# Three of four sums of weight blocks and one low part move from GpSimd to VectorE in the gate and up projection of layer 1

## The chip, the cores and the metric

The kernel runs on one core of a Trainium2 chip. A core has TensorE (matrix products into PSUM), VectorE and ScalarE (which read PSUM and SBUF), GpSimd (SBUF alone) and SyncE, whose queue issues the loads here. The metric is the device time of one execution in microseconds, the median of the timed runs. In the rows PE is TensorE, PEld its loading of weights, DVE is VectorE, ACT is ScalarE, POOL is GpSimd and SP is SyncE.

## The reference

A two-layer backbone over 512 latent tokens and 256 context tokens, model width 1024. Each layer has a mixer and a SwiGLU feed-forward part, both between norms and modulations. The change lies in the gate and up products of the second layer's feed-forward part, which exists for the latent tokens alone:

```
D_FF = 2816                     # 22 blocks of 128 columns
def swiglu(u, w_gate, w_up, w_down):
    return (jax.nn.silu(u @ w_gate) * (u @ w_up)) @ w_down
...
    f = swiglu(modulate(rms_norm(h, g_pre_ffn[i]), sh_f, sc_f), w_ffn_gate[i], w_ffn_up[i], w_ffn_down[i])
    h = h + gt_f * rms_norm(f, g_post_ffn[i])
```

## The kernel before

All products are in fp32 accuracy, made of three passes: each operand is split into a high part (a ScalarE copy to the rounded format, line 181) and a low part (operand minus high part, line 182, on VectorE unless another engine is given). The three passes are high by high, high by low and low by high (lines 197 to 199).

The gate and up products use Winograd's form of Strassen's scheme: for a pair of weight row blocks and a pair of token blocks, 7 products take the place of 8. The sums on the token side (tile `ub`) are made while the tokens are normalised (`norm_W`, `Winograd.add`, lines 1440 to 1475). The sums on the weight side are made in `gate_up`, `group`, for each two of the 22 column blocks, once for the gate weights (m = 0) and once for the up weights (m = 1): 22 groups, which take turns gate, up, gate, up. A group does this:

- two loads of 512 KB bring four blocks of weights, 128 rows by 512: a11, a12, a21, a22 (tile `raw_gu`, four buffers, so two groups);
- four sums of them: s1 = a21 + a22, s2 = s1 - a11, s4 = a12 - s2, s3 = a11 - a21 (tile `s`, four buffers in turn, so the sums of one group), lines 1556 to 1559, all on GpSimd;
- seven products, of a11, a12, s1, s4, s3, s2 and a22. For each the high part is made on ScalarE and the low part on VectorE; the low part of s3 alone is made on GpSimd. Each product is 4 x 3 matmuls;
- the products come out of PSUM by one ScalarE copy (line 1551) and seven additions on VectorE that read PSUM and SBUF (lines 1552 and 1562 to 1567);
- `done`: for the gate, ScalarE applies silu (line 1617); for the up weights GpSimd multiplies gate and up, two operations (line 1615).

The variable `n` is the number of columns of one product: 384 in layer 0 (768 tokens, six blocks, three pairs) and 256 in layer 1 (512 tokens, two pairs). `wide` is true for n <= 256, so in layer 1 alone; there two products share one PSUM bank.

The order on each queue isn't the order of the text. A planner simulates the engines with costs of its own and issues what is ready, earlier lines first. Each engine then runs its queue strictly in order, and a semaphore wait holds what stands behind it.

Of the kernel before, what the change touches and what calls it, by code (L numbers as in the profile page):

```python
# [155 lines left out]
ALU = mybir.AluOpType  # L156
# [7 lines left out]
def emit(tc, A):  # L164
    nc = tc.nc
    V, S, G, T = nc.vector, nc.scalar, nc.gpsimd, nc.tensor
# [29 lines left out]
    def mm3(out, wh, wl, xh, xl, start, stop):  # L196
        T.matmul(out, wh, xh, start=start, stop=False)  # L197
        T.matmul(out, wh, xl, start=False, stop=False)  # L198
        T.matmul(out, wl, xh, start=False, stop=stop)  # L199
# [220 lines left out]
    def pacc(name="pacc"):  # L420
        return bank_of(("g", "g", "g", "s", "s", "po"), name)

    def ptp(name="ptp"):
        return bank("v", name)

    def wraw(nm):
        return wp.tile([128, RK, 512], F32, tag="raw", name="raw_" + nm, bufs=RB)

    def wsplit(src, nm, lo_eng=None):
        hi, lo = [wp.tile([128, 512], F32R, tag=x_, name=f"{x_}_{nm}") for x_ in ("hi", "lo")]  # L430
        n = src.shape[1]
        split(hi[:, :n], lo[:, :n], src, lo_eng)
        return hi[:, :n], lo[:, :n]
# [1086 lines left out]
    def gate_up(U, pairs, wg, wu, place, done, lead):  # L1520


        n = pairs * 128
        wide = n <= 256
        v3 = lambda ap: ap.rearrange("p (i c) -> p i c", c=128)
        def group(f, m, w):
            def rows(f, n):
                raw = wraw("gu")
                nc.sync.dma_start(raw.rearrange("p (f j) c -> p f (j c)", f=n), w[f:f + n].rearrange("f p c -> p f c"))
                return [raw[:, i, :] for i in range(2 * n)]  # L1530

            a11, a12, *low = rows(f, RK // 2)
            banks = {}

            def prod(i, a, b, lo_eng=None):

                n_ = i // 2 if wide else i
                if n_ not in banks:
                    banks[n_] = ptp("st") if i == 6 and not wide else pacc("st")
                ps = banks[n_][:, i % 2 * 256:i % 2 * 256 + n] if wide else banks[n_][:, :n]  # L1540
                hi, lo = wsplit(a, "gu", lo_eng)
                for q in range(4):
                    ks = slice(q * 128, (q + 1) * 128)
                    uh_, ul_ = U.moving(b, q)
                    mm3(v3(ps), hi[:, ks], lo[:, ks], uh_, ul_, q == 0, q == 3)
                return v3(ps)

            p1, q_ = [v3(x) for x in U.sums_of_products()]
            c = place(f, m)
            P1, P2 = prod(0, a11, 0), prod(1, a12, 4)  # L1550
            S.activation(p1, P1, AF.Copy)
            V.tensor_tensor(c[0][0], p1, P2, ALU.add)
            yield
            a21, a22 = low or rows(f + 1, 1)
            s1, s2, s3, s4 = [U.sums.tile([128, 512], F32, tag="sum", name=f"s{i}", bufs=4) for i in range(4)]
            G.tensor_tensor(s1, a21, a22, ALU.add)  # L1556
            G.tensor_tensor(s2, s1, a11, ALU.subtract)
            G.tensor_tensor(s4, a12, s2, ALU.subtract)
            G.tensor_tensor(s3, a11, a21, ALU.subtract)
            P5, P3 = prod(3, s1, 1), prod(2, s4, 5)  # L1560
            P7, P6 = prod(4, s3, 2, G), prod(5, s2, 3)
            V.tensor_tensor(q_, p1, P6, ALU.add)
            V.tensor_tensor(p1, q_, P5, ALU.add)
            V.tensor_tensor(c[0][1], p1, P3, ALU.add)
            V.tensor_tensor(c[1][1], p1, P7, ALU.add)
            V.tensor_tensor(q_, q_, P7, ALU.add)
            V.tensor_tensor(c[1][0], q_, prod(6, a22, 6), ALU.add)
            done(f, m)

        lag = Lagged(lead)  # L1570
        for f in range(0, KF, 2):
            for m, w in enumerate((wg, wu)):
                with tc.issue_after(U.turned.ins) if 0 < f + m < lead else ExitStack():
                    lag.add(group(f, m, w))
                if f + m + 1 >= lead:
                    lag.flush()
# [644 lines left out]
```

## Time and profile before

| what | value |
|---|---|
| median of 3 runs | 2040.51 us |
| the three runs | 2040.86, 2040.51, 2028.3 us |
| the profiled execution | 2035.29 us |
| its span, first to last instruction | 2033.5 us |
| granted TensorE clock, mean | 0.955 |
| gate and up stage of layer 1 | about 1655 to 1905 us of the span |

The profile is one execution. Busy time counts an instruction from start to end, so it includes the time in which a started instruction is held up. The times of rows are microseconds from the start of the span.

### The profile page before, as it was taken

Reading aid. Unit: us, or ns where it says so; the run is one execution under the profiler, and the core shown is the slowest. Engines: PE = TensorE matmul, PEld = TensorE weight load, DVE = VectorE, ACT = ScalarE, POOL = GpSimd, SP = SyncE. Lnnn points to the kernel's source line nnn. Section 1 sums busy time; section 2 is a strip of 40 time slices with the busy share of each in tenths; the row PEclk is TensorE's granted clock in tenths of the full one; section 3 lists DMA queues with packets and bytes.
Section 4 is the critical chain, followed back from the end, with each engine's and each line's share of the span. In section 5 each row is a group of like instructions: output and inputs, shape, how many; then the busy total and the mean of one; then the engine's idle time right before and its main releaser. Section 6 shows DMA issues by size and latency. Waiting matters only on the chain. (4 is left out here: it accounts for less than half of the span.)

```text
span 2033.5 us, 33984 instructions
## 1 busy us (share of the span) xinstructions
PE 1844.2 (91%) x12852; PEld 1524.8 (75%) x12852; DVE 1449.5 (71%) x1973; ACT 962.5 (47%) x1806; POOL 1063.3 (52%) x936
## 2 busy tenths in 40 slices
PE   5989977888898969999999999889989969999998
PEld 3977754655566869999997777677755659999886
DVE  3687757667876696666666876887566679999754
ACT  3433456666864553333343235523455445444443
POOL 1276455344523376656548555656246358888201
PEclk8999988998999979999999889999999979999999
DMA  8255595655734613221227433586524202333331
GB/s 304 68 152 142 180 285 162 186 161 163 230 92 142 235 62 105 78 83 63 74 91 255 156 119 99 171 271 217 169 90 133 94 21 88 100 96 102 105 103 63
DMA packets 125728, 280.19 MB, mean 138 GB/s; under 512 B 12870, under 2 KB 43474, under 8 KB 125564
## 3 DMA queue, kind: packets, MB, share of 16 engines
q1 hardware_dynamic: 125564, 278.02, 43.5%
q8 instruction: 101, 1.65, 0.3%
q14 instruction: 63, 0.52, 0.1%
HBM read 226.14 MB, written 46.07 MB: 134 GB/s over the span
## 5 line engine op out<-in xcount | busy, mean ns | idle before, releaser
L197 PE MATMUL st<-ub,hi_gu 128*128 128x384 f32 (+1 forms) x1232 | 384.2, 312 | 18.0 <-ACT ub L181 18.0
L199 PE MATMUL st<-ub,lo_gu 128*128 128x384 f32 (+1 forms) x1232 | 385.5, 313 | 11.3 <-POOL lo_gu L182 9.5
L198 PE MATMUL st<-ub,hi_gu 128*128 128x384 f32 (+1 forms) x1232 | 384.0, 312 | 1.8 <-DVE ub L182 1.8
L197 PEld LDWEIGHTS st<-ub,hi_gu 128*128 128x128 f32 x1232 | 233.9, 190 | 18.9 <-ACT ub L181 18.9
L199 PEld LDWEIGHTS st<-ub,lo_gu 128*128 128x128 f32 x1232 | 233.7, 190 | 15.3 <-POOL lo_gu L182 11.6
L198 PEld LDWEIGHTS st<-ub,hi_gu 128*128 128x128 f32 x1232 | 233.8, 190 | 2.5 <-DVE ub L182 2.5
L181 ACT ACTIVATE hi_gu<-s 128x512 fp32r<-128x512 f32 x176 | 110.9, 631 | 191.0 <-PE st L198 141.8
L182 DVE TENSOR_TENSOR lo_gu<-raw_gu,hi_gu 128x512 fp32r<-128x512 f32 x132 | 161.5, 1237 | 39.9 <-ACT hi_gu L181 39.9
L182 DVE TENSOR_TENSOR lo_gu<-s,hi_gu 128x512 fp32r<-128x512 f32 x132 | 151.4, 1148 | 44.5 <-ACT hi_gu L181 44.1
L1649 PE MATMUL dn<-hi_wd,gh 128*128 128x512 f32 x440 | 174.5, 399 | 2.2 <-ACT gh L181 2.2
L1650 PE MATMUL dn<-lo_wd,gh 128*128 128x512 f32 x440 | 174.9, 398 | 0.8 <-DVE lo_wd L182 0.8
L1651 PE MATMUL dn<-hi_wd,gl 128*128 128x512 f32 x440 | 165.7, 403 | 6.1 <-POOL gl L182 5.1
L254 DVE SCALAR_TENSOR_TENSOR macc<-mraw,cs,macc 128x1024 f32<-128x1024 f32 x80 | 123.4, 1564 | 22.4 <-DMA mraw<-in_wmb_dram 13.5
L182 DVE TENSOR_TENSOR lo_wd<-raw_wd,hi_wd 128x512 fp32r<-128x512 f32 x110 | 99.4, 910 | 47.4 <-ACT hi_wd L181 47.3
L181 ACT ACTIVATE hi_gu<-raw_gu 128x512 fp32r<-128x512 f32 x132 | 81.8, 629 | 96.7 <-PE st L198 88.7
L1556 POOL TENSOR_TENSOR s<-raw_gu 128x512 f32<-128x512 f32 x44 | 57.3, 1302 | 133.0 <-DVE lo_gu L182 100.3
L181 ACT ACTIVATE gh<-g 128x512 fp32r<-128x512 f32 x76 | 47.6, 630 | 122.3 <-PE dn L1650 103.2
L860 ACT ACTIVATE P<-st 128x512 f32<-128x512 f32 x128 | 73.1, 596 | 67.2 <-PE st L199 28.3
L1651 PEld LDWEIGHTS dn<-hi_wd,gl 128*128 128x128 f32 x440 | 83.2, 191 | 28.3 <-POOL gl L182 7.9
L1649 PEld LDWEIGHTS dn<-hi_wd,gh 128*128 128x128 f32 x440 | 84.2, 191 | 22.4 <-ACT gh L181 2.7
L1650 PEld LDWEIGHTS dn<-lo_wd,gh 128*128 128x128 f32 x440 | 83.9, 191 | 20.8 <-DVE lo_wd L182 1.3
L1104 ACT ACTIVATE cu<-Y 64x512 f16<-64x512 f32 x120 | 70.7, 589 | 19.6 <-PE Y L1158 17.8
(539 smaller groups left out, 4917.8 us busy)
## 6 DMA issues: line engine op xcount, KB each, us to landing
mraw<-in_wmb_dram SPq DMA_DIRECT2D x56, 512.0 KB, 4.2
raw_wd<-in_wd_dram SPq DMA_DIRECT2D x55, 512.0 KB, 3.5
raw_gu<-in_wg_dram SPq DMA_DIRECT2D x44, 512.0 KB, 3.4
raw_gu<-in_wu_dram SPq DMA_DIRECT2D x44, 512.0 KB, 3.6
cu<-in_wmb_dram SPq DMA_DIRECT2D x24, 512.0 KB, 5.0
raw_m<-in_wmb_dram SPq DMA_DIRECT2D x16, 512.0 KB, 5.0
raw_qkv<-in_wqkv_dram SPq DMA_DIRECT2D x12, 512.0 KB
raw_tok<-qk_d SPq DMA_DIRECT2D x12, 512.0 KB
```

What stands on the lines that cost most here:

```text
L181: S.activation(hi, src, AF.Copy)
L182: (lo_eng or V).tensor_tensor(lo, src, hi.bitcast(F32), ALU.subtract)
L197: T.matmul(out, wh, xh, start=start, stop=False)
L198: T.matmul(out, wh, xl, start=False, stop=False)
L199: T.matmul(out, wl, xh, start=False, stop=stop)
L254: V.scalar_tensor_tensor(a, raw, cs[:, self.k, v:v + 1], a, ALU.mult, ALU.add)
L860: S.activation(P[:, :n], ps[:, :n], AF.Exp)
L1104: S.activation(diag(Y, p), r3(py)[half(p)], AF.Copy)
L1556: G.tensor_tensor(s1, a21, a22, ALU.add)
L1649: T.matmul(ps, gh[:, tsl], wh, start=start, stop=False)
L1650: T.matmul(ps, gh[:, tsl], wl, start=False, stop=False)
L1651: T.matmul(ps, gl_[:, tsl], wh, start=False, stop=stop)
```

## The change

`adder` is VectorE where `wide` is true and GpSimd elsewhere. It makes the sums s1, s2 and s4 and the low part of s3. The sum s3 stays on GpSimd. Layer 0 isn't changed.

```diff
             s1, s2, s3, s4 = [U.sums.tile([128, 512], F32, tag="sum", name=f"s{i}", bufs=4) for i in range(4)]
-            G.tensor_tensor(s1, a21, a22, ALU.add)
-            G.tensor_tensor(s2, s1, a11, ALU.subtract)
-            G.tensor_tensor(s4, a12, s2, ALU.subtract)
+            adder = V if wide else G
+            adder.tensor_tensor(s1, a21, a22, ALU.add)
+            adder.tensor_tensor(s2, s1, a11, ALU.subtract)
+            adder.tensor_tensor(s4, a12, s2, ALU.subtract)
             G.tensor_tensor(s3, a11, a21, ALU.subtract)
             P5, P3 = prod(3, s1, 1), prod(2, s4, 5)
-            P7, P6 = prod(4, s3, 2, G), prod(5, s2, 3)
+            P7, P6 = prod(4, s3, 2, adder), prod(5, s2, 3)
```

## Rows read from the trace of the kernel before

**Rows 1.** The page's head and its busy time by engine.
```profile
span 2033.5 us, 33984 instructions
...
PE 1844.2 (91%) x12852; PEld 1524.8 (75%) x12852; DVE 1449.5 (71%) x1973; ACT 962.5 (47%) x1806; POOL 1063.3 (52%) x936
```
**Rows 2.** Busy time by window: length, then PE, PEld, DVE, ACT, POOL, clock, DMA share, GB/s.
```profile
1690.00:1716.00 26.00, 26.00 (x221) 26.00 (x220) 25.59 (x31) 13.33 (x24) 22.09 (x16) 1.00 0.26 83
...
1720.00:1900.00 180.00, 170.40 (x1400) 167.05 (x1400) 176.85 (x220) 85.66 (x152) 143.67 (x98) 1.00 0.31 97
```
**Rows 3.** TensorE's waits, 1720 to 1900 us: total, times, longest.
```profile
PE st L199 <- POOL lo_gu L182: 7.7, 8, 1.0
PE st L199 <- DVE lo_gu L182: 1.9, 8, 0.3
```
**Rows 4.** The chain that ended last, from 1767 us: start, length, what.
```profile
1767.61 1.24 POOL lo_gu L182
1768.90 0.39 PE st L199
```
**Rows 5.** Timeline of VectorE from 1759 us: start, duration (of all instructions merged), instruction.
```profile
1759.43 3.14 DVE L182 TENSOR_TENSOR lo_gu<-raw_gu,hi_gu 128x512 fp32r<-128x512 f32 x2
1762.50 1.77 DVE L182 TENSOR_TENSOR lo_gu<-s,hi_gu 128x512 fp32r<-128x512 f32 x1
1764.20 0.40 DVE L1562 TENSOR_TENSOR p<-p,st 128x256 f32<-128x256 f32 x1
1764.64 0.42 DVE L1563 TENSOR_TENSOR p<-p,st 128x256 f32<-128x256 f32 x1
...
1766.11 0.41 DVE L1564 TENSOR_TENSOR up<-p,st 128x256 f32<-128x256 f32 x1
1766.44 0.41 DVE L1565 TENSOR_TENSOR up<-p,st 128x256 f32<-128x256 f32 x1
...
1769.32 0.68 DVE L182 TENSOR_TENSOR lo_gu<-raw_gu,hi_gu 128x512 fp32r<-128x512 f32 x1
1769.92 0.41 DVE L1552 TENSOR_TENSOR up<-p,st 128x256 f32<-128x256 f32 x1
...
1781.08 3.13 DVE L182 TENSOR_TENSOR lo_gu<-raw_gu,hi_gu 128x512 fp32r<-128x512 f32 x2
```
**Rows 6.** Timeline of GpSimd in the same pair of groups.
```profile
1760.29 1.74 POOL L1558 TENSOR_TENSOR s<-raw_gu,s 128x512 f32<-128x512 f32 x1
...
1766.32 1.29 POOL L1557 TENSOR_TENSOR s<-s,raw_gu 128x512 f32<-128x512 f32 x1 [0.68 <-PE st L199]
1767.58 1.27 POOL L182 TENSOR_TENSOR lo_gu<-s,hi_gu 128x512 fp32r<-128x512 f32 x1
```
**Rows 7.** Groups of VectorE, 1720 to 1900 us: count, busy us, mean ns, idle before.
```profile
L182 DVE TENSOR_TENSOR lo_gu<-raw_gu,hi_gu 128x512 fp32r<-128x512 f32 x49 | 70.6, 1465 | 0.5 <-ACT hi_gu L181 0.5
L182 DVE TENSOR_TENSOR lo_gu<-s,hi_gu 128x512 fp32r<-128x512 f32 x51 | 70.5, 1382 | 0.3
```
**Rows 8.** Timelines of GpSimd and TensorE at the start of the stage.
```profile
1656.92 1.28 POOL L1557 TENSOR_TENSOR s<-s,raw_gu 128x512 f32<-128x512 f32 x1
...
1659.87 1.71 POOL L182 TENSOR_TENSOR lo_gu<-s,hi_gu 128x512 fp32r<-128x512 f32 x1
...
1664.66 1.71 POOL L1558 TENSOR_TENSOR s<-raw_gu,s 128x512 f32<-128x512 f32 x1
...
1669.31 0.58 PE L197 MATMUL st<-ub,hi_gu 128*128 128x256 f32 x1 [8.64 <-ACT ub L181]
```
**Rows 9.** GpSimd's waits, 1720 to 1900 us: total, times, longest.
```profile
POOL s L1556 <- DVE lo_gu L182: 14.9, 16, 1.3
POOL s L1557 <- PE st L199: 8.9, 13, 0.7
POOL s L1558 <- DVE lo_gu L182: 5.5, 8, 0.7
```

## The prediction, on record before the change was run

> **What bounds the kernel now.** I read the page first: TensorE is busy 91% of a span of 2033.5 us and VectorE 71% [rows 1]. Those are means over many stages, and the edit touches only one of them: the test `wide` is true where a block has at most 256 columns, which is layer 1 (two pairs of token blocks); layer 0 has 384 columns and keeps GpSimd. So I went to the stretch in which layer 1's gate and up products run, about 1655 to 1905 us, and cut it into windows [rows 2]. From 1690 to 1716 us TensorE never stops and passes 221 matmuls in 26.0 us, 0.1176 us each. From 1720 to 1900 us it passes 1400 in 180 us; at 0.1176 us these need 164.7 us, so 15.3 us are lost. VectorE is busy 176.85 of those 180 us, GpSimd 143.67. The waits of TensorE in the same stretch name the losers' partners: 8 long waits (up to 1.0 us) for the low part that GpSimd writes, 8 short ones for a low part of VectorE [rows 3]; the rest of the 15.3 us is the slower restart behind each wait. The chain of waits shows the long one in place: GpSimd's low part ends, then TensorE starts [rows 4].
>
> The unit of the stage is one pair of groups (gate and up of the same two weight columns). The same instruction of VectorE comes back after 1781.08 - 1759.43 = 21.65 us [rows 5]. A pair has 2 x 7 products x 4 blocks x 3 passes = 168 matmuls, 168 x 0.1176 = 19.76 us. So a pair is 1.89 us longer than TensorE needs, over 180/21.65 = 8.3 pairs 15.7 us, near the 15.3 above.
>
> Why is VectorE full? Its low part takes 0.68 us when GpSimd is quiet and 1.77 us when it isn't; to the next start it is 0.60 us in the first case (1769.32 to 1769.92) and 1.70 in the second (1762.50 to 1764.20) [rows 5]. GpSimd's own operation takes 1.28 to 1.30 us beside VectorE's sums of PSUM and SBUF and up to 1.7 us otherwise [rows 6], and those sums keep 0.41 us beside it [rows 5]. So the operations of VectorE with both inputs in SBUF take turns with GpSimd's, one whole instruction each, and one collision costs VectorE 1.70 - 0.60 = 1.10 us. The 100 low parts of the 180 us take 70.6 + 70.5 = 141.1 us [rows 7]; at 0.68 us they would take 68.0. VectorE therefore spends 73.1 us, 8.8 us a pair, waiting for GpSimd, and that shows as busy time. GpSimd has 98 operations there [rows 2], so each costs VectorE 0.746 us on average: about two in three collide fully.
>
> **The change part by part.** Removed from GpSimd, per pair: three sums twice and one low part twice, 8 of its 12 operations. Added to VectorE: the same 8 operations, 128x512, two SBUF inputs, as its low parts are. Own time of VectorE in a pair now: 21.65 - 8.8 = 12.85 us (this holds its short idle time too). The 8 added ones cost the 0.60 us that an undisturbed low part occupies: 4.8 us; together 17.65 us. That the sums follow each other (s1, s2, s4) I take at nothing: the trace has a dependent pair of VectorE at 0.44 us between starts (1764.20, 1764.64) against 0.33 for an independent one (1766.11, 1766.44) [rows 5], so at most 4 x 0.11 = 0.44 us a pair, and only where nothing stands between.
>
> What stays on GpSimd is the sum s3 and the product of gate and up, 4 operations a pair. Their cost to VectorE isn't shown for the new order, so it has bounds: 0 if all run beside the PSUM sums, 4 x 1.10 = 4.4 us if each collides. I take today's mean, 4 x 0.746 = 3.0 us: one of the two products can start once line 1564 is done and then runs beside lines 1565 to 1567, which want no turn; the others have no such cover. VectorE needs 17.65 + 3.0 = 20.65 us a pair, with ends 17.65 and 22.05. TensorE's 19.76 lies between them.
>
> So VectorE stays the bound, but a shorter one: 20.65 instead of 21.65. TensorE comes into the stage with a lead: VectorE's cycle is 21.65 us from 1687 us on, and TensorE shows its first stall only at about 1716 us, 1.33 pairs later, so the lead is 1.33 x 1.89 = 2.5 us. After the change it falls back 20.65 - 19.76 = 0.89 us a pair, and the lead lasts 2.8 pairs. From 1687 to 1902 us there are 9.9 pairs; the other 7.1 lose 0.89 us each, 6.3 us in all, against 15.3 now. Gain: 9.0 us.
>
> The wait that goes is the one for GpSimd's low part: it sat in GpSimd's queue behind s2 (1766.32, ends 1767.61) and took 1.27 us more [rows 6]; on VectorE it is one turn of 0.60 us. What is late next is VectorE's own low part, the short wait of [rows 3].
>
> The start, 1655 to 1676 us, is another matter: there the last token block is normalised on VectorE and GpSimd in turns, while TensorE waits 8.64 us [rows 8]. Three operations of the second group stand between them on GpSimd (1656.92, 1659.87, 1664.66, [rows 8]), 1.3 to 1.7 us each. Moved, they free up to 3 x 1.10 = 3.3 us and cost VectorE 3 x 0.60 = 1.8 us: 1.5 us gained. Both ends: if they fill only idle time of VectorE, 3.3 us gained; if they are queued in front of the normalisation and add their 1.8 us to the wait without freeing anything, 1.8 us lost. The first group's sums lie earlier, where VectorE has time.
>
> No transfer is added or moved. The two loads of a group wait for s3 and the low parts, which come no later; SP's queue keeps its order. On VectorE's queue the sums do bring new waits (for the raw load, and for the buffer of the sum before), with the low parts and the PSUM sums queued behind them; that is priced among the rivals. ScalarE's high parts, now often late behind GpSimd's sums, come earlier, and at 85.66 busy of 180 us it has room [rows 2].
>
> The sum: 9.0 + 1.5 = 10.5 us. Against the profiled execution (2035.29 us, of which 2033.5 are the span) that is 2024.8. The three timed runs are 2028.3, 2040.5 and 2040.9 us, so the profiled one lies inside their spread of 12.5 us; the middle of all four is 2037.9, and 2037.9 - 10.5 = 2027.4. I forecast 2027 us.
>
> One rule speaks against the change. VectorE is busy 98% of the stretch and GpSimd 80% [rows 2], so by occupancy work goes the wrong way. The Trainium skill, page "Perfetto Trace Analysis", section "Optimizing Scalar/DVE Operations", says that with VectorE saturated it may make sense to hand some of its work to ScalarE or even GpSimd, and adds that between VectorE and GpSimd this might not help since they share a read port. By its first half the 8 operations would cost their present mean, and the time would be that of the fourth rival; the turns in [rows 5] bear out the second half.
>
> **The rivals.**
> First, TensorE becomes the bound: the four GpSimd operations cost VectorE under 19.76 - 17.65 = 2.1 us a pair, 0.53 us each. For it: VectorE's slack lets GpSimd run in gaps, and nearly free GpSimd starts the product early, beside the PSUM sums. Against it: today's mean is 0.746. It gives the whole 15.3 us and 1.5 at the start: 16.8 us, 2021.
>
> Second, all four collide: 22.05 us a pair, 0.40 longer than now, 9.9 pairs, 4.0 us, less the 1.5 at the start: 2.5 us slower, 2040. For it: once the wait of s3 for its buffer ends with a low part of VectorE, s3 starts straight into the next one. Against it: VectorE's 14 PSUM sums a pair need no turn.
>
> Third, slower outright: a sum at the head of VectorE's queue waits and holds up everything behind it. On GpSimd the sums waited for 14.9 + 8.9 + 5.5 = 29.3 us in 180 us [rows 9], 3.5 us a pair, and hurt only GpSimd. If VectorE took over these waits whole, a pair would need 20.65 + 3.5 = 24.15 us, 2.5 more than now, 9.9 pairs, 24.8 us less 1.5: 2061 us. It decides from a wait of 1.0 us a pair on. Against it: 20.4 of the 29.3 us were waits for a low part of VectorE, which an earlier place in the same queue satisfies, and the 0.68 us gaps between s1 and s2 are GpSimd's own, since s2 needs s1.
>
> Fourth, the added operations cost their present mean: 8 x 1.41 = 11.3 us a pair, 9.9 pairs, 112 us slower, 2150. Against it: the excess of a low part over 0.68 us is paid once for each GpSimd operation, and those fall from 12 to 4.
>
> That the change moves nothing is excluded, as the 8 operations are plain assignments to an engine. But the order on every queue is planned anew around them, so s1 or s4 may stand elsewhere than I assume; the bounds above hold that.
>
> **How the numbers follow.** Forecast 0.46, TensorE as the bound 0.28, all collide 0.18, head of the queue 0.06, mean cost 0.02. For this kernel a difference under 1%, 20 us, can hardly be told from none. Faster by over 1% needs the first rival with 3.3 us at the start or the spread of runs besides: 0.12. Slower by over 1%: the last two rivals, 0.07 (rounded). The rest, 0.81, is within 1%. The range: from the fastest run shown with the first rival's gain, 2028.3 - 16.8 = 2011, to the slowest with the second rival's steady loss, 2040.9 + 4.0 = 2045; the last two rivals stay outside, and about as much again for the spread.
>
> **What would show it.** The low part on VectorE should have a mean nearer 0.9 us than 1.41; the same instruction should return after about 20.6 us; GpSimd should be busy about a third of its present time in this stretch; TensorE's waits for GpSimd's low part should be gone, and 1720 to 1900 us should hold about 1480 matmuls (180/0.1176 = 1531 would be the first rival). The forecast is wrong if a pair takes 21.65 us or more, if VectorE shows idle time in front of lines 1556 to 1558 that ends with a load or with ScalarE, or if the start of the stage moves by more than 3 us.

## The result, and the profile after

The changed kernel takes 2045.43 us (median of 20 runs, 2036.77 to 2049.61), the kernel before 2033.62 us (20 runs, 2027.02 to 2040.86). The ratio is 1.0053, 95% interval 1.0040 to 1.0066: 10.8 us slower by the ratio (the medians lie 11.8 us apart), where 10.5 us faster was forecast. The profiled execution has a span of 2039.2 us against 2033.5, only 5.7 us more, because its earlier stages, whose code is the same, ran some 8 us faster: the last eight transposes ahead of the gate and up stage start at 1648.61 us, before at 1656.72. From their start to the first matmul of the down projection (1910.08 us, before 1903.19) it is 261.5 us, before 246.5. The stage itself is 15.0 us longer.

Line numbers are higher by one from 1557 on: s1, s2 and s4 are lines 1557 to 1559, s3 is 1560, the additions 1563 to 1568.

The window that answers to [rows 2], in the same columns:
```profile
1720.00:1900.00 180.00, 161.15 (x1298) 156.10 (x1297) 160.76 (x264) 77.91 (x140) 51.31 (x32) 1.00 0.30 90
```
GpSimd's busy time fell from 143.67 to 51.31 us, as meant. But TensorE passes 1298 matmuls instead of 1400, and VectorE, which was idle for 3.15 us, is now idle for 19.2 of 180 us. The groups of VectorE, against [rows 7], show in front of what:
```profile
L182 DVE TENSOR_TENSOR lo_gu<-raw_gu,hi_gu 128x512 fp32r<-128x512 f32 x48 | 47.8, 1021 | 0.0
L182 DVE TENSOR_TENSOR lo_gu<-s,hi_gu 128x512 fp32r<-128x512 f32 x62 | 47.5, 766 | 0.0
L1559 DVE TENSOR_TENSOR s<-raw_gu,s 128x512 f32<-128x512 f32 x16 | 19.7, 1229 | 0.0
L1557 DVE TENSOR_TENSOR s<-raw_gu 128x512 f32<-128x512 f32 x15 | 10.4, 692 | 19.2 <-DMA raw_gu<-in_wg_dram 9.9 <-DMA raw_gu<-in_wu_dram 9.3
```
All of it stands in front of s1 and ends with a load: 15 times, 1.28 us each. The low parts themselves fell to a mean of 0.87 us from 1.41. The timeline of VectorE over one such wait (start, duration, instruction, idle time before it and its end):
```profile
1766.26 1.78 DVE L182 TENSOR_TENSOR lo_gu<-raw_gu,hi_gu 128x512 fp32r<-128x512 f32 x1
1767.97 0.41 DVE L1552 TENSOR_TENSOR up<-p,st 128x256 f32<-128x256 f32 x1
1768.30 1.28 DVE L182 TENSOR_TENSOR lo_gu<-raw_gu,hi_gu 128x512 fp32r<-128x512 f32 x2
1769.50 0.68 DVE L182 TENSOR_TENSOR lo_gu<-s,hi_gu 128x512 fp32r<-128x512 f32 x1
1770.10 0.41 DVE L1563 TENSOR_TENSOR p<-p,st 128x256 f32<-128x256 f32 x1
1771.70 0.69 DVE L1557 TENSOR_TENSOR s<-raw_gu 128x512 f32<-128x512 f32 x1 [1.19 <-DMA raw_gu<-in_wu_dram]
...
1774.24 1.33 DVE L182 TENSOR_TENSOR lo_gu<-s,hi_gu 128x512 fp32r<-128x512 f32 x1
...
1780.40 0.41 DVE L1552 TENSOR_TENSOR up<-p,st 128x256 f32<-128x256 f32 x1
```
The first of these lines is the low part of a22, the last reader of its buffer. The chain that ended last shows what hangs on it:
```profile
1768.07 3.54 DMA raw_gu<-in_wu_dram
1771.70 0.69 DVE s L1557
...
1774.32 1.26 DVE lo_gu L182
1775.63 0.39 PE st L199
```
At 1768.04 us the low part of a22 ends and its buffer is free; the load that goes into it starts at 1768.07 and lands after 3.54 us; s1, the sum that reads it, is at the head of VectorE's queue from 1770.51 (1770.10 + 0.41) on and stands there for 1.19 us, and the low parts behind s1 reach TensorE late. TensorE's waits, against [rows 3]:
```profile
PE st L199 <- DVE lo_gu L182: 18.7, 20, 1.7
```
The wait for GpSimd's low part is gone. A longer one, for VectorE, stands in its place.

Line 1552 came at 1757.18 us two groups earlier, so a pair takes 1780.40 - 1757.18 = 23.2 us, against 21.65 in [rows 5]. From 1699.2 to 1897.4 us this line comes back 17 times, which gives 23.3 us a pair in the mean.

### The profile page after: what moved, and what is told of

The parts are those of the page before. It is cut to its first block, busy times and chain, and to the rows that moved or that the text cites. A ratio compares the mean times of both kernels' runs of the same rounds, so it can differ in the third digit from the quotient of the medians.

```text
span 2039.2 us, 33992 instructions
## 1 busy us (share of the span) xinstructions
PE 1843.8 (90%) x12852; PEld 1522.6 (75%) x12852; DVE 1442.4 (71%) x2061; ACT 961.2 (47%) x1806; POOL 935.7 (46%) x848
## 5 line engine op out<-in xcount | busy, mean ns | idle before, releaser
L197 PE MATMUL st<-ub,hi_gu 128*128 128x384 f32 (+1 forms) x1232 | 384.2, 312 | 19.1 <-ACT ub L181 19.1
L182 DVE TENSOR_TENSOR lo_gu<-s,hi_gu 128x512 fp32r<-128x512 f32 x154 | 130.9, 850 | 44.4 <-ACT hi_gu L181 44.4
L182 DVE TENSOR_TENSOR lo_gu<-raw_gu,hi_gu 128x512 fp32r<-128x512 f32 x132 | 134.6, 1033 | 37.1 <-ACT hi_gu L181 37.1
L1560 POOL TENSOR_TENSOR s<-raw_gu 128x512 f32<-128x512 f32 x44 | 71.4, 1622 | 118.5 <-DVE lo_gu L182 97.3
L1616 POOL TENSOR_TENSOR g<-g,up 128x512 f32<-128x512 f32 x38 | 55.7, 1466 | 103.3 <-DVE up L1565 72.8
```

The costliest lines, as they stand in the source:

```text
L182: (lo_eng or V).tensor_tensor(lo, src, hi.bitcast(F32), ALU.subtract)
L1616: G.tensor_tensor(g, g, u, ALU.mult)
```

## The experiments

Two theories. **A, the late load:** four buffers serve the loads of two groups, so the load for s1 reuses the buffer that the low part of a22 two groups earlier has just left. VectorE reaches s1 before it lands, and stands. **B, VectorE and its port** (the turns that it takes with GpSimd): VectorE is full, 8 more operations a pair are too many, and the wait for the load only fills time that would be lost anyway. All comparisons are with the kernel before on the same chip; "the stage" is the time from the start of the last eight transposes to the first matmul of the down projection, in the one profile of each kernel, 246.5 us before.

### One more buffer

```diff
-                raw = wraw("gu")
+                turn_u[0] += 1
+                if wide and turn_u[0] % 5 >= 4:
+                    raw = U.more.tile([128, RK, 512], F32, tag="more", name="raw_gu", bufs=1)
+                else:
+                    raw = wraw("gu")
...
+    U1.more = pool("more", ph_u)
```


> The changed kernel with five buffers for the weight loads of layer 1's gate and up stage in place of four (the fifth from the space that the output projection has left). Theory A, the late load: in the changed kernel VectorE stands 1.2 us a group, 2.4 us a pair, in front of s1, for a load whose buffer the low part of a22, six instructions earlier on the same queue, has just set free; with a fifth buffer that load reuses one that is free some 5 us earlier. The wait should vanish, a pair go from 23.2 to about 20.8 us, and the time to about 8 us under the kernel before (ratio 0.996). Theory B, VectorE and the port: the wait only fills time that VectorE would lose to GpSimd or TensorE anyway; a pair stays over 22.5 us and the ratio at 1.004 or more.

2020.12 us against 2035.56, ratio 0.9926 (0.9911 to 0.9940); the stage took 235.4 us. The window, and VectorE's rows at two places a pair apart (line 1562 is s1 here):
```profile
1720.00:1880.00 160.00, 159.55 (x1329) 158.28 (x1328) 159.97 (x268) 80.05 (x141) 54.50 (x32) 1.00 0.33 102
```
```profile
1755.32 0.41 DVE L1568 TENSOR_TENSOR p<-p,st 128x256 f32<-128x256 f32 x1
1755.65 0.68 DVE L1562 TENSOR_TENSOR s<-raw_gu 128x512 f32<-128x512 f32 x1
...
1775.59 0.41 DVE L1568 TENSOR_TENSOR p<-p,st 128x256 f32<-128x256 f32 x1
1775.92 0.68 DVE L1562 TENSOR_TENSOR s<-raw_gu 128x512 f32<-128x512 f32 x1
```
No idle time stands in front of s1, a pair takes 1775.59 - 1755.32 = 20.27 us, and TensorE is busy for 159.55 of 160 us. Theory B, with 1.004 or more, falls: the operations on VectorE are the same. The gain of 15 us was larger than the 8 us that theory A gave (20.8 us a pair); the stage shows 11.1 of the 15 us.

### The same buffer in the kernel before

The same edit, on the kernel before.

> The kernel before with the same fifth buffer, as a control: GpSimd's wait for the load was hidden there behind its wait for the buffer of the sum, so theory A expects no change (ratio 0.998 to 1.002, a pair at 21.65 us). If the buffer by itself makes the kernel faster by 0.4% or more, a gain of the run before can't be put down to the wait on VectorE.

2035.41 us, ratio 0.9991 (0.9976 to 1.0006). A pair takes 21.65 us as before, so the buffer alone is worth nothing; with the change it moves the ratio from 1.0053 to 0.9926. Here it pays only where a sum waits on VectorE's queue.

### The low part alone

```diff
-            P7, P6 = prod(4, s3, 2, G), prod(5, s2, 3)
+            P7, P6 = prod(4, s3, 2, V if wide else G), prod(5, s2, 3)
```


> The kernel before with only the low part of s3 moved to VectorE; all four sums stay on GpSimd. No sum stands on VectorE's queue, so theory A expects no wait for a load there. VectorE's own time grows by 1.2 us a pair and two of twelve collisions (0.75 us each) go, so a pair should stay within 0.5 us of 21.65 and TensorE lose its 1 us wait for GpSimd: ratio 0.995 to 1.001. Theory B (any operation added to the full VectorE costs): 1.2 us a pair and more, ratio 1.005.

2028.31 us, ratio 0.9958 (0.9939 to 0.9976); the stage took 241.0 us. By itself the low part, a quarter of the moved operations, brings a gain, where theory B expected a loss. VectorE doesn't wait for a load once, and a pair takes 21.0 us, a little under what was expected (21.15 to 22.15). GpSimd now waits for the loads, in front of s1, and that costs little (its groups, 1720 to 1880 us, idle time last):
```profile
L1556 POOL TENSOR_TENSOR s<-raw_gu 128x512 f32<-128x512 f32 x15 | 20.7, 1381 | 28.4 <-DMA raw_gu<-in_wu_dram 18.8 <-DVE p L1563 5.2 <-DVE lo_gu L182 4.4
```

### The three sums alone

```diff
-            P7, P6 = prod(4, s3, 2, adder), prod(5, s2, 3)
+            P7, P6 = prod(4, s3, 2, G), prod(5, s2, 3)
```


> The changed kernel with the low part of s3 back on GpSimd: three sums on VectorE. Theory A expects the wait for the load in front of s1 to be there as in the changed kernel, about 1.2 us a group, and the ratio at 1.003 to 1.008. Theory B expects a gain against the changed kernel, as VectorE has 1.2 us less of its own a pair: ratio 1.000 or lower.

2041.61 us, ratio 1.0034 (1.0022 to 1.0045). The wait is there, 20.5 us in 160, 1.37 us a group:
```profile
L1557 DVE TENSOR_TENSOR s<-raw_gu 128x512 f32<-128x512 f32 x15 | 10.4, 692 | 20.5 <-DMA raw_gu<-in_wg_dram 10.8 <-DMA raw_gu<-in_wu_dram 9.7
```
So the sums alone bring the wait and the loss, as theory A expected. But the low part, a gain by itself, is none on top of the sums: without it a pair takes 22.3 us against 23.3, and the stage 253.8 us against 261.5, in one profile of each (the ratios, 1.0034 and 1.0053, are too close to tell them apart). The wait is about as long in both, 1.37 and 1.28 us a group. A likely reason, not tested by itself, is that VectorE's own time comes on top of a wait that it doesn't fill; so far theory B has a part.

### The product of a22 first

No buffer is added; the changed kernel only computes the last product of the second part first, so that the low part of a22 is made early.
```diff
+            P4 = prod(6, a22, 6)
             P5, P3 = prod(3, s1, 1), prod(2, s4, 5)
...
-            V.tensor_tensor(c[1][0], q_, prod(6, a22, 6), ALU.add)
+            V.tensor_tensor(c[1][0], q_, P4, ALU.add)
```


> The changed kernel with four buffers as it is, but with the product of a22 put in front of the products of s1, s4, s3 and s2 in each group's second part. The low part of a22 is the last reader that sets the late load's buffer free; made first, it frees the buffer some 5 us earlier, with no memory added. Theory A, the late load: the wait in front of s1 goes, a pair falls to 20 to 21 us, ratio to the kernel before 0.991 to 0.997, as with the fifth buffer. Rival, more room for loads as such helps (not the moment at which this one buffer is freed): no gain over the changed kernel, ratio 1.004 or more.

2020.46 us against 2036.35, ratio 0.9919 (0.9900 to 0.9938); the stage took 235.7 us. From 1720 to 1880 us VectorE is busy without a break, and no wait of TensorE is left:
```profile
1720.00:1880.00 160.00, 159.93 (x1343) 159.39 (x1342) 160.00 (x273) 82.90 (x144) 45.96 (x33) 1.00 0.32 106
```
So what counts is the moment at which this buffer is freed; a fifth buffer isn't needed for it.

### s1 back on GpSimd

```diff
-            adder.tensor_tensor(s1, a21, a22, ALU.add)
+            G.tensor_tensor(s1, a21, a22, ALU.add)
```


> The changed kernel with s1, the one sum that stands in front of the queue waiting for the load, back on GpSimd; s2, s4 and the low part of s3 stay on VectorE, four buffers. Theory A: the wait for the load moves to GpSimd's queue, where it holds up little; GpSimd has 6 operations a pair and VectorE 6 fewer than 8 added ones, own time 16.45 us and 6 collisions of 0.75 to 1.0 us: a pair of 20.9 to 22.4 us, ratio 0.995 to 1.002, under the changed kernel's 1.005. Rival, the chain of sums is on the path wherever it stands: VectorE then waits for GpSimd in front of s2, ratio 1.004 or more.

2036.13 us, ratio 1.0001 (0.9982 to 1.0019). The wait for the load is off VectorE (GpSimd now has 19.1 us of it in 160), and the loss with it, but a smaller wait takes its place, in front of s2, which now needs s1 from GpSimd: 10.3 us in 160.
```profile
L1558 DVE TENSOR_TENSOR s<-s,raw_gu 128x512 f32<-128x512 f32 x15 | 17.9, 1190 | 10.3 <-POOL s L1557 10.3
```
Theory A and the rival of this run both have a part: moving s1 removes the loss, and the chain of sums holds back some of the gain.

### All four sums on VectorE

```diff
-            G.tensor_tensor(s3, a11, a21, ALU.subtract)
+            adder.tensor_tensor(s3, a11, a21, ALU.subtract)
```


> The changed kernel with s3 on VectorE too, four buffers: GpSimd keeps only the products of gate and up, two operations a pair. VectorE gains 2 x 0.60 us of its own and loses two collisions of about 1.0 us. Theory A: the wait in front of s1 for the load stays, 0.8 us a group or more, a pair of 22.2 to 23.2 us, ratio 1.001 to 1.006. Rival, the port: with GpSimd nearly out of the way the gain shows, ratio 0.998 or lower.

2031.12 us, ratio 0.9967 (0.9950 to 0.9985). This was a miss for theory A's number, and the rival's condition, 0.998 or lower, came true: a pair takes 21.2 us. The wait stayed, but it shrank, to 12.9 us in 160, 0.86 us a group:
```profile
L1557 DVE TENSOR_TENSOR s<-raw_gu 128x512 f32<-128x512 f32 x15 | 10.4, 693 | 12.9 <-DMA raw_gu<-in_wu_dram 7.3 <-DMA raw_gu<-in_wg_dram 5.6
```
The timeline shows why (line 1560 is s3):
```profile
1766.25 0.69 DVE L182 TENSOR_TENSOR lo_gu<-raw_gu,hi_gu 128x512 fp32r<-128x512 f32 x1
1766.86 0.42 DVE L1552 TENSOR_TENSOR up<-p,st 128x256 f32<-128x256 f32 x1
1767.19 0.69 DVE L1560 TENSOR_TENSOR s<-raw_gu 128x512 f32<-128x512 f32 x1
...
1770.71 0.69 DVE L1557 TENSOR_TENSOR s<-raw_gu 128x512 f32<-128x512 f32 x1 [0.70 <-DMA raw_gu<-in_wu_dram]
```
s3 stands between the low part of a22 and s1, in the time that VectorE spent waiting, so most of its 0.60 us costs nothing; and on GpSimd it had collided with the low part of a22 (1.78 us in the changed kernel, 0.69 here), which the next load into that buffer waits for. So the collisions with GpSimd have their part in the loss, through the late load. I had charged s3 as if VectorE had no gap.

### All four sums and one more buffer

The edits of the last and of the first experiment together.

> All four sums and all low parts on VectorE and the fifth buffer for the loads. Theory A: no wait for a load; VectorE's own time about 18.1 us a pair and two collisions, up to 2.2 us: 18.9 to 20.3 us, so TensorE's 19.8 or VectorE bounds; ratio 0.990 to 0.994, the same as three sums with the fifth buffer (0.9926) or slightly under it. If VectorE's own 1.2 us more a pair decide, 0.994 to 0.997.

2019.00 us, ratio 0.9912 (0.9895 to 0.9930); the stage took 234.9 us.
```profile
1720.00:1880.00 160.00, 160.00 (x1336) 160.00 (x1335) 157.81 (x286) 82.86 (x143) 23.19 (x16) 1.00 0.34 102
```
TensorE is busy the whole time and VectorE has slack again: in this window TensorE is the bound. The three versions without the wait (0.9926, 0.9919, 0.9912) can't be told apart, and all three beat both kernels.

The medians stand up to 6 us lower than the stage's own change gives (a22 first: 15.9 us under the kernel before, its stage 10.8); the changed kernel too is 10.8 us slower by the ratio, its stage 15.0. The part behind the stage gives about 1 us of that in some of the profiles (2033.5 - 1903.2 = 130.3 us before, 129.1 in the changed kernel); the rest can't be read from one profile of each and stays open.

## Why the prediction was wrong

**The step that failed** is the wait at the head of VectorE's queue, which the 20.65 us a pair put at nothing. The reason given was "The two loads of a group wait for s3 and the low parts, which come no later", and with it the third rival, a sum at the head of VectorE's queue, got 0.06. That rival is what happened, and its place was right: VectorE stood idle in front of s1 for 2.47 us a pair (19.2 us over 180/23.2 = 7.76 pairs), where the rival had priced 3.5. But its price was taken from [rows 9], which hold no wait for a load, so that the two sizes are near is luck. Two of the prediction's own signs of being wrong came: a pair of more than 21.65 us, and idle time in front of s1 that ends with a load.

Two readings misled me. First, I set the rival aside because [rows 9] put 20.4 of 29.3 us of GpSimd's waits down to a low part of VectorE. Such a row names only what came last of several. The load had come just ahead of it: in the kernel before, SyncE's queue shows two issues in one row, each 0.33 us long,
```profile
1763.75 6.61 SPq L1529 DMA_DIRECT2D raw_gu<-in_wu_dram  x2
```
so the second of the two starts at 1763.75 + 6.61 - 0.33 = 1770.03 us. If it lands after 3.4 us (the median of this stage's loads in that trace, 3.4 to 3.5), it is there at 1773.4. GpSimd began s1 at 1774.07:
```profile
1774.07 1.29 POOL L1556 TENSOR_TENSOR s<-raw_gu 128x512 f32<-128x512 f32 x1 [1.23 <-DVE lo_gu L182]
```
The load had about 0.6 us to spare, under a wait with another name. With the low part alone moved, that other wait is shorter, and 18.8 us of GpSimd's waits in front of s1 end with a load.

Second, "come no later" is beside the point: what shrank is the time that covers the load. Before, the low part of a22 ended at 1770.00 (1769.32 + 0.68, [rows 5]) and s1 began 4.07 us later. Two of the four operations of VectorE in between, the two of the first row, were stretched by collisions with GpSimd:
```profile
1770.25 3.14 DVE L182 TENSOR_TENSOR lo_gu<-raw_gu,hi_gu 128x512 fp32r<-128x512 f32 x2
1773.31 0.68 DVE L182 TENSOR_TENSOR lo_gu<-s,hi_gu 128x512 fp32r<-128x512 f32 x1
```
After, the same two take 1.28 us (the row at 1768.30), and s1's turn comes 2.47 us after the low part of a22 (1768.04 to 1770.51), sooner than the load. The change removed these collisions, and they had hidden the load. I asked of each stall what is late next, but only on the compute engines.

**The terms of the sum**, per pair: own time of VectorE 17.65 us forecast; 16.95 is what is left of the measured 23.2 less the wait of 2.47 and the collisions. Collisions 3.0 us forecast; 29.3 us over 32 GpSimd operations (the low parts and s4 less 0.68 us each), 0.916 each, 3.8 us a pair measured, between the forecast and the second rival's 4.4. The sum of the two, 20.65 forecast, is 20.7. That it fits so well is luck, as the errors of the two terms cancel; but without the wait a pair takes 20.27 us in the first experiment, so VectorE's load was sound in size. The missing term was the wait.

**The effect on TensorE:** 102 matmuls fewer in 180 us. Over the stretch of 9.9 pairs, 23.2 - 21.65 = 1.55 us each is 15.3 us, and the stage is 15.0 us longer.

**The start** was forecast 1.5 us shorter and is nearly unchanged: from the start of the last transposes to the stage's first sum of products (line 1562 before, 1563 after) it is 23.4 us before and 23.8 after; TensorE's long wait there is 9.75 us against 8.64 [rows 8].

**TensorE's floor** was put too low: 221 matmuls in 26 us [rows 2] count those cut off at both edges. The long stretches without a wait, 1336 in 160.0 us with all sums on VectorE and one more buffer and 1343 in 159.93 us with a22 first, give 0.1198 and 0.1191 us each, 20.0 to 20.1 us a pair and not 19.76. At 0.1198 us the kernel before lost 12.3 us in its 180 us and not 15.3. TensorE's first wait there also stands later than the prediction has it, at 1724.6 us (0.96 us long) and not at 1716, so the lead was longer. Neither slip turns the forecast around. The chances of the last two rivals add up to 0.08, not 0.07.

**The fourth rival** is excluded as argued: the low parts' mean fell to 0.87 us. VectorE at 98% could take the work: with the load out of the way the same move gains 0.7%, and the low part alone 0.4%. By its excess over 0.68 us a low part, 73 of its 177 busy us were time in which GpSimd held it up. The Trainium skill, page "Perfetto Trace Analysis", section "Optimizing Scalar/DVE Operations", says that it may make sense to hand work of a saturated VectorE to other engines; the runs here speak against that half of its advice.

## What to carry to other kernels

A step that moves to another queue takes its waits along, and in a strict order everything behind it waits too: look up when each of its inputs is really there, also those that another wait hid. Compare a load's time to landing with what stands between the release of its buffer and the reader. Where a change takes out collisions or other slow instructions, ask what those were hiding. A load that comes just too late can be mended by the order in which its buffer's readers run, as well as by another buffer.

## What the runs showed of the hardware that I had not expected

Fewer operations on GpSimd collided harder: the cost to VectorE of each rose from 0.746 to 0.916 us when 98 operations in 180 us became 32, so a share of collisions read from a crowded stretch isn't a constant. And a collision has a place: the 1.1 us on the low part of a22 (1.78 us in the changed kernel, 0.69 with all four sums on VectorE) also put off the load into that buffer.
